# A hybrid attention and DeltaNet layer: weights kept until used, diagonal blocks copied whole, scan products by column halves

## The chip, the cores and the metric

The kernel runs on one core of one Trainium2 chip, as one program. A core has five engines with an instruction stream each: TensorE (PE) for matrix products, with a separate stream of weight loads (PEld); VectorE (DVE); ScalarE (ACT); GpSimd (POOL); SyncE (SP). Each of them takes its instructions in the order in which they stand. SP, ACT and POOL also issue DMA transfers, and a transfer that waits for its data holds up what stands behind it in that queue. The metric is the device time of one execution in microseconds (us); lower is better.

## The reference

One layer of an encoder for 1024 tokens of width 1024. After a conditioned RMSNorm, one projection gives the inputs of two mixers: attention over 8 heads, and a gated DeltaNet with 8 heads that is scanned forwards and backwards in 16 chunks of 64 tokens. A mixture of 16 experts follows. What the change touches is the chunked DeltaNet:

```python
L = where(strict, (kb @ k.T) * decay, 0)          # 64x64, one per chunk, head and direction
T = triangular_solve(eye + L, eye)                # its inverse
u = T @ vb;  w = T @ (kb * exp(gc))
a_intra = where(incl, (q @ k.T) * decay, 0)
...
def step(state, inp):                             # scan over the 16 chunks
    v_new = u_n - w_n @ state
    o_n = qg_n @ state + a_n @ v_new
    state = state * gl_n + kd_n.T @ v_new
```

Both directions run, their outputs are summed, and the sum goes through a gated RMSNorm per head.

## The kernel before

All projections are three products of split weights and activations: `wh`, the rounded weights, with `hTh` and with `hTl`, and `wl`, what the rounding lost, with `hTh`. `proj_load` (L271) asks for a block of 128 columns (`wraw`, a DMA on POOL's queue), rounds it on ACT (`wh`, L278) and subtracts on DVE (`wl`, L279). `wraw`, `wh` and `wl` have two buffers each. A block costs PE 48 products of 128x512 (L285; L1152 in the late filler), and its result leaves through ACT.

The mixer goes through these stages:

1. The DeltaNet's projections, with convolution and normalisation (`dn_group`).
2. `dn_tile` for eight tiles of two chunks: products of keys with keys and with queries (L481), decays (rr on DVE, L489 on PE, the exponential on ACT), and per direction the matrix `at` (stored to `a_d`) and the matrix `nn` (stored to `n_d`, L503). `dn_blocks` then fetches the two 32x32 diagonal blocks of every 64x64 matrix of `n_d` into `nb`, by four DMAs on ACT's queue for each half of the tiles (L511), a row of 32 numbers at a time. Between the tiles stand three projection blocks of queries and keys (`qkv_group`).
3. `dn_invert`: the inverses of all diagonal blocks at once on DVE, 31 steps of two products (L536) and two subtractions (L540), whose size is `q(32-q)` for step `q` in each of two blocks. PE meanwhile has eight projection blocks, `qkv_group` 3 to 5 and `gate_group` 0 to 4 (called gate 0 to gate 4 below). A loop asks for the next block's weights before each:

```python
for n, (f, c, g) in enumerate(fills):
    if n + 1 < len(fills):
        with self.tc.high_priority(offset=0):
            self.proj_ahead(fills[n + 1][1] + fills[n + 1][2] * 128)
    f(g)
```

   `proj_ahead` (L288) keeps a single pair in `self.ahead`. The call for block n+1 comes ahead of block n's use, so it overwrites the pair that was kept for n, and `proj` loads, rounds and subtracts that block a second time. Of the 14 loads of this loop, six are never used.
4. The scan, 16 steps, step t with chunk t forwards and chunk 15-t backwards. `scan_merge` makes the off-diagonal 32x32 blocks of the inverse (L611, L618, 32x32 products, with transposes on DVE, L608). `scan_step` has the products of keys and queries with the state (L633, 128x128, four for each direction), two products on DVE (L636) and two subtractions (L640), the product with the inverse (L645), the state's update (L660, L663, copies on ACT, L666) and the outputs (L670, then sums on DVE, L676 to L679). Between these PE works through the late filler (L1152, 15 blocks), the rotary preparation (`attn_prep`) and the conditioning vector (`mods`).
5. Attention, the merge, the router and the experts.

The order within each engine is set at build time by a list scheduler, from priorities and its own cost estimates; only `dn_invert`'s steps are held in their written order.

## Time and profile before

| | us |
|---|---|
| median of 3 runs | 1736.34 (1730.99 to 1738.34) |
| the profiled execution | 1736.07, its span 1733.9 |
| tile stage | 214 to 291 |
| inversion on DVE | 305.75 to 375.1 |
| last projection block ahead of the late filler ends | 386.2 |
| scan | 408 to 710, late filler until 729 |
| attention, merge, router, experts | to the end |

Over the span PE is busy for 93%, DVE for 84%, ACT for 53%, POOL for 12%; the mean granted TensorE clock is 0.971. These shares are means over very different stages, so a stage has to be read by itself: which engine works without a gap in it, and what the other engines wait for. A busy share of PE includes the time in which a product only drains; how fast PE goes is better read from the distance between the starts of neighbouring rows.

### The profile page before, as it was taken

The numbers are of one execution on the slowest core, as the hardware profiler recorded it, in microseconds if no ns is written. First come the engines' busy times: TensorE is split into PE (matmuls) and PEld (weight loads), VectorE is DVE, ScalarE is ACT, GpSimd is POOL, SyncE is SP. The second block draws the span as 40 slices with busy tenths as digits, with TensorE's granted clock in tenths as the row PEclk, the third lists the DMA queues.
The fourth block names the chain that finished last, engine by engine and source line by source line (L and its number), as shares of the span: only waits on it lengthen the run. The fifth ranks groups of instructions, "written<-read, shape, count | busy, mean of one in ns | idle before, by whom it ended". The sixth has DMA issues, their size and how long they took to land. (4 is left out here: it accounts for less than half of the span.)

```text
span 1733.9 us, 28593 instructions
## 1 busy us (share of the span) xinstructions
PE 1615.1 (93%) x10363; PEld 1287.0 (74%) x10363; DVE 1454.2 (84%) x2523; ACT 924.5 (53%) x1382; POOL 211.9 (12%) x191
## 2 busy tenths in 40 slices
PE   5999998398999999999999999859999999999997
PEld 4777877277777777778887788647777777777776
DVE  6899896966887778889986477979999999999997
ACT  6654522123333323488881223337777777777775
POOL 0011001011111100021113222210010100110000
PEclk9999999699999899999999999969999999999999
DMA  9466479256877876521126463769999999999981
GB/s 279 127 178 187 110 205 221 68 174 174 213 211 189 253 192 159 167 71 37 36 74 202 141 230 128 272 213 345 386 383 371 383 386 383 382 373 382 386 324 25
DMA packets 283052, 390.81 MB, mean 225 GB/s; under 512 B 78299, under 2 KB 151695, under 8 KB 282655
## 3 DMA queue, kind: packets, MB, share of 16 engines
q1 hardware_dynamic: 247103, 328.15, 57.3%
q0 software_dynamic: 12960, 47.19, 9.9%
q10 hardware_dynamic: 22848, 13.63, 2.9%
q8 instruction: 82, 1.34, 0.3%
q14 instruction: 59, 0.48, 0.1%
HBM read 330.14 MB, written 58.77 MB: 224 GB/s over the span
## 5 line engine op out<-in xcount | busy, mean ns | idle before, releaser
L1519 DVE TENSOR_TENSOR ew<-er,ew 128x1024 fp32r<-128x1024 f32 x384 | 452.2, 1220 | 29.8 <-ACT ew L1518 29.8
L1518 ACT CAST ew<-er 128x1024 fp32r<-128x1024 f32 x384 | 391.0, 1048 | 137.9 <-PE pj L1572 108.1
L1572 PE MATMUL pj<-ew,xT 128*128 128x512 f32 x1536 | 367.6, 396 | 4.6 <-DVE ew L1519 4.6
L1572 PEld LDWEIGHTS pj<-ew,xT 128*128 128x128 f32 x1536 | 283.2, 188 | 76.1 <-DVE ew L1519 19.4
L1589 PE MATMUL tr<-ew,aT 128*128 128x512 f32 x768 | 191.4, 398 | 0.0
L1589 PEld LDWEIGHTS tr<-ew,aT 128*128 128x128 f32 x768 | 139.7, 188 | 30.5 <-DVE ew L1519 3.5
L285 PE MATMUL pj<-hTh,wl 128*128 128x512 f32 (+1 forms) x368 | 117.7, 398 | 26.1 <-DVE wl L279 26.1
L285 PE MATMUL pj<-hTh,wh 128*128 128x512 f32 (+1 forms) x368 | 117.2, 398 | 3.6 <-ACT hTh L258 1.8
L285 PE MATMUL pj<-hTl,wh 128*128 128x512 f32 (+1 forms) x368 | 118.6, 399 | 1.4 <-DVE hTl L261 1.4
L278 ACT CAST wh<-wraw 128x1024 fp32r<-128x1024 f32 (+1 forms) x45 | 46.7, 1038 | 126.9 <-PE pj L285 61.1
L285 PEld LDWEIGHTS pj<-hTh,wl 128*128 128x128 f32 (+1 forms) x368 | 69.1, 188 | 43.0 <-DVE wl L279 26.6
L275 POOL DMA_DIRECT2D wraw<-in_w_in_dram x42 | 37.6, 896 | 417.3 <-DVE wl L279 282.3
L1595 POOL DMA_INDIRECT out_dram<-xe,idxT x16 | 37.1, 2316 | 408.5 <-DVE tok L1493 354.0
L841 DVE TENSOR_REDUCE am<-pj 128x1 f32<-128x1024 f32 x64 | 77.8, 1218 | 10.6 <-PE pj L836 10.0
L1198 PE MATMUL pj<-hTh,uw 128*128 128x512 f32 x256 | 83.5, 404 | 1.0 <-DVE uth L1204 0.5
L1152 PE MATMUL pj<-hTh,wh 128*128 128x512 f32 x240 | 82.9, 416 | 0.6 <-ACT y L1157 0.4
L285 PEld LDWEIGHTS pj<-hTh,wh 128*128 128x128 f32 (+1 forms) x368 | 67.9, 187 | 19.6 <-ACT hTh L258 1.9
L1152 PE MATMUL pj<-hTl,wh 128*128 128x512 f32 x240 | 82.1, 411 | 0.0
L1152 PE MATMUL pj<-hTh,wl 128*128 128x512 f32 x240 | 82.1, 410 | 0.0
L285 PEld LDWEIGHTS pj<-hTl,wh 128*128 128x128 f32 (+1 forms) x368 | 68.4, 188 | 17.5 <-DVE hTl L261 2.0
L836 PE MATMUL pj<-kT,qT 128*128 128x512 f32 x256 | 74.9, 403 | 2.3 <-ACT ap L843 1.2
L843 ACT ACTIVATE ap<-pj,am 128x1024 f32<-128x1024 f32 x64 | 72.0, 1125 | 6.7 <-DVE am L841 5.7
(378 smaller groups left out, 3010.1 us busy)
## 6 DMA issues: line engine op xcount, KB each, us to landing
er<-in_w_gate_dram SPq DMA_DIRECT2D x128, 512.0 KB, 7.0
er<-in_w_up_dram SPq DMA_DIRECT2D x128, 512.0 KB
er<-in_w_down_dram SPq DMA_DIRECT2D x128, 512.0 KB, 9.9
wraw<-in_w_in_dram POOLq DMA_DIRECT2D x42, 512.0 KB, 5.9
mw<-in_w_ada_dram SPq DMA_DIRECT2D x64, 256.0 KB, 5.2
wt<-in_w_ada_dram SPq DMA_DIRECT2D x16, 512.0 KB, 8.0
gate_d<-y ACTq DMA_DIRECT2D x32, 256.0 KB, 2.8
kqs<-kq_d SPq DMA_DIRECT2D x32, 256.0 KB, 5.7
```

What stands on the lines that cost most here:

```text
L275: (queue or nc.gpsimd).dma_start(raw[:, :, :n], self.i["w_in"][0, :, col:col + n].rearrange("(k p) c -> p k c", p=128))
L278: nc.scalar.copy(wh[:, :, :n], raw[:, :, :n])
L285: self.nc.tensor.matmul(ps[q][:n], w[:, k, :n], x[k][:, q * 512:(q + 1) * 512], start=(k == 0 and w is wh and x is self.hTh), stop=(k == 7 ...
L836: nc.tensor.matmul(ps[:, kh], qT[:, i * 128:(i + 1) * 128], self.kT[a][:, s, kh * 512:(kh + 1) * 512], start=(s == 0), stop=(s == 1), skip ...
L841: nc.vector.reduce_max(m, ps, axis=AX.X, negate=True)
L843: nc.scalar.activation(p, ps, AF.Exp, bias=m, scale=1.0, accum_out=self.rv[:, h, half * 4 + i:half * 4 + i + 1])
L1152: nc.tensor.matmul(ps[q], a[:, k], x[k][:, q * 512:(q + 1) * 512], start=(k == 0 and a is wh and x is self.hTh), stop=(k == 7 and a is wl))
L1198: nc.tensor.matmul(ps, w[:, k], v[k][:, qs], start=(k == 0 and p == 0), stop=(k == 3 and p == 2))
L1518: nc.scalar.copy(hi, raw)
L1519: nc.vector.tensor_sub(lo, raw, hi.bitcast(F))
L1572: nc.tensor.matmul(pg[m], x[:, 2 * kp + k], wi[:, k], start=(kp == 0 and k == 0 and n == 0), stop=(kp == 3 and k == 1 and n == 2))
L1589: nc.tensor.matmul(py[q], x[:, k], wi[:, q], start=(k == 0 and n == 0), stop=(k == 7 and n == 2))
```

## The change

`self.ahead` becomes a table by column, so a block that was asked for ahead is held until it is used; the eight blocks of stage 3 are loaded once each, the first of them already during the tile stage. Each tile's `nn` goes to DRAM in pieces: the diagonal blocks to `nb_d` (SP, four DMAs for each tile and direction), the one off-diagonal block that is needed to `n_d` (POOL, two). `dn_blocks` fetches whole 8 KB rows of `nb_d` on POOL's queue, after every second tile, in place of ACT's queue. The memset of the inverses moves from POOL to DVE. The transposed diagonal blocks are made once on ACT and stored to `wt_d`, and the scan loads them in place of transposing on DVE. In the scan, the products with the state are split by column halves so that both directions share a PSUM tile: 16 products of 64 columns in place of 8 of 128. Multiplication, subtraction and the sum of outputs are then one instruction for both directions. Outputs are kept by pairs of chunks (t, 15-t), and one output pair is finished in each of the steps 8 to 15.

```diff
     def proj_ahead(self, col):
-        self.ahead = col, self.proj_load(col)
+        self.ahead[col] = self.proj_load(col)
...
-        if self.ahead and self.ahead[0] == col:
-            wh, wl = self.ahead[1]
-            self.ahead = None
-        else:
-            wh, wl = self.proj_load(col, n)
+        wh, wl = self.ahead.pop(col, None) or self.proj_load(col, n)
...
             for x in range(2):
-                nc.sync.dma_start(self.n_d[d, 2 * j + x].rearrange("h s c -> s h c"),
-                                  nn[64 * x:64 * x + 64].rearrange("p (h c) -> p h c", c=64))
+                n = 2 * j + x
+                rows = lambda b, e: nn[64 * x + 32 * b:64 * x + 32 * b + 32].rearrange(
+                    "p (h c) -> p h c", c=64)[:, :, 32 * e:32 * e + 32]
+                for b in range(2):
+                    nc.sync.dma_start(self.nb_d[d, 8 * n:8 * n + 8, b].rearrange("h s c -> s h c"), rows(b, b))
+                nc.gpsimd.dma_start(self.n_d[d, n].rearrange("h s c -> s h c"), rows(d, 1 - d))
...
-            src = self.n_d[d, 2 * j0:2 * j1].rearrange("n h (b s) c -> (n h) b s c", b=2)
-            for b in range(2):
-                self.nc.scalar.dma_start(self.nb[d][16 * j0:16 * j1, b], src[:, b, :, b * 32:b * 32 + 32])
+            self.nc.gpsimd.dma_start(self.nb[d][16 * j0:16 * j1].rearrange("p b s c -> p (b s c)"),
+                                     self.nb_d[d, 16 * j0:16 * j1].rearrange("n b s c -> n (b s c)"))
...
-            nc.gpsimd.memset(w, 0.0)
+            nc.vector.memset(w, 0.0)
...
             nc.sync.dma_start(self.w_d[d], ws[d].rearrange("p b s c -> p (b s c)"))
+            nc.scalar.copy(tmps[d][:, 0], ws[d][:, d].rearrange("p s c -> p c s"))
+            nc.scalar.dma_start(self.wt_d[d], tmps[d][:, 0].rearrange("p c s -> p (c s)"))
...
-        for f, o, cf, co in quads:
-            nc.vector.transpose(wt[f], w[f, :, cf])
...
-        for d, n in enumerate(ns):
-            pk = self.pa.tile([128, 8, 64], F, name="dn", bufs=2)
+        tq = self.tq
+        pk = [self.pa.tile([128, 8, 64], F, name="dn", bufs=2) for _ in range(2)]
+        for y, rows in zip(pk, (rs, os)):
             for p in range(4):
-                nc.tensor.matmul(pk[:, 2 * p:2 * p + 2, :].rearrange("p h c -> p (h c)"), kq[d][:, p],
-                                 self.St[:, d, p, :], start=True, stop=True, skip_group_check=True)
...
+                for d, r in enumerate(rows):
+                    nc.tensor.matmul(y[r, 2 * p:2 * p + 2, :].rearrange("p h c -> p (h c)"), kq[d][:, p, r],
+                                     self.St[:, d, p, :], start=True, stop=True, skip_group_check=True)
+        eg = lambda s: self.egs[:, s, t].unsqueeze(2).to_broadcast([128, 8, 64])
+        nc.vector.tensor_mul(x, pk[0], eg(0))
+        nc.vector.tensor_sub(x, kv[:, 1].rearrange("p (h c) -> p h c", c=64), x)
+        nc.vector.tensor_mul(tq, pk[1], eg(1))
...
-            begin(self.in_turn(self.scan_post(j) for j in range(NT) if max(2 * j + 1, 15 - 2 * j) == t))
+            if t > 7:
+                begin(self.scan_post(15 - t))
...
                     self.dn_tile(j)
-                    if j == 5:
-                        self.dn_blocks(0, 4)
-                self.dn_blocks(4, NT)
+                    if j == QKV[-1]:
+                        self.proj_ahead(C_Q + len(QKV) * 128)
+                    if j in (2, 4, 6):
+                        self.dn_blocks(j - 2, j)
+                self.dn_blocks(6, NT)
```

DVE, between the last tile and the first steps of the inversion: before, with the products on `nb` at L536.

```order
L501 TENSOR_TENSOR nn<-dn,e 128x4x64 x2
L279 TENSOR_TENSOR wl<-wraw,wh 128x1024 x2
L523 MEMSET wb_2752 128x32 x2
L523 MEMSET wb_2757 128x32 x2
L536 TENSOR_TENSOR wtmp_2756<-nb_707,wb_2752 128x2x31
L912 TENSOR_SCALAR macc<-mw_711,cs 128x512
L279 TENSOR_TENSOR wl<-wraw,wh 128x1024
L536 TENSOR_TENSOR wtmp_2761<-nb_708,wb_2757 128x2x31
```

The same place of the changed kernel (its lines 506, 528, 531, 544 are 501, 520, 523, 536 of before; 908 is 902):

```order
L506 TENSOR_TENSOR nn<-dn,e 128x4x64 x2
L279 TENSOR_TENSOR wl<-wraw,wh 128x1024
L528 MEMSET wb_2829 128x2048
L528 MEMSET wb_2834 128x2048
L531 MEMSET wb_2829 128x32 x2
L531 MEMSET wb_2834 128x32 x2
L544 TENSOR_TENSOR wtmp_2833<-nb_709,wb_2829 128x2x31
L908 TENSOR_TENSOR y<-y,tr 1x512
L544 TENSOR_TENSOR wtmp_2838<-nb_710,wb_2834 128x2x31
```

Three `wl` (gate 0's and two that are never used) stand ahead of the second direction's first step before, one (gate 0's) now; two large memsets and the addition L908 have come in.

DVE, around gate 1's `wl` within the inversion (the last two numbers of a shape give the step: 16x16 is step 16), before:

```order
L540 TENSOR_TENSOR wb_2752<-wb_2752,wtmp_2756 128x2x16x16
L540 TENSOR_TENSOR wb_2757<-wb_2757,wtmp_2761 128x2x16x16
L279 TENSOR_TENSOR wl<-wraw,wh 128x1024
L536 TENSOR_TENSOR wtmp_2756<-nb_707,wb_2752 128x2x15x17
L536 TENSOR_TENSOR wtmp_2761<-nb_708,wb_2757 128x2x15x17
```

and now:

```order
L548 TENSOR_TENSOR wb_2829<-wb_2829,wtmp_2833 128x2x19x13
L548 TENSOR_TENSOR wb_2834<-wb_2834,wtmp_2838 128x2x19x13
L279 TENSOR_TENSOR wl<-wraw,wh 128x1024
L544 TENSOR_TENSOR wtmp_2833<-nb_709,wb_2829 128x2x18x14
L544 TENSOR_TENSOR wtmp_2838<-nb_710,wb_2834 128x2x18x14
```

Gate 1's `wl` has moved from behind step 16 to behind step 13; the next three stand behind steps 16, 19 and 22.

PE, a middle step of the scan, from the merge's L618 to the product with the inverse (L645), before:

```order
L618 MATMUL tr<-W,pt 32x32 x16
L1152 MATMUL pj<-hTh_404,wl 128x512
L149 MATMUL tr<-masks,hl 128x128 x4
L1152 MATMUL pj<-hTh_445,wh 128x512
L633 MATMUL dn<-St,kqs 128x128 x2
L149 MATMUL tr<-masks,kk 128x128 x4
L633 MATMUL dn<-St,kqs 128x128 x2
L149 MATMUL tr<-masks,qraw 128x128 x4
L645 MATMUL dn<-st,W 64x64
```

and the same step now (628, 1163, 644 and 657 are 618, 1152, 633 and 645 of before):

```order
L628 MATMUL tr<-W,pt 32x32 x16
L1163 MATMUL pj<-hTh_611,wl 128x512
L149 MATMUL tr<-masks,hl 128x128 x4
L1163 MATMUL pj<-hTh_652,wh 128x512
L644 MATMUL dn<-St,kqs 64x128 x3
L149 MATMUL tr<-masks,kk 128x128 x4
L644 MATMUL dn<-St,kqs 64x128 x11
L149 MATMUL tr<-masks,qraw 128x128 x4
```

The products with the state, full size before, are now two runs of half size between full-size work, and all of a step's stand ahead of the next L645.

## Rows read from the trace of the kernel before

**Rows 1.** Busy time by stage: us (instructions) per engine, granted clock, DMA share.

```profile
core 0: us, PE busy (x) PEld busy (x) DVE busy (x) ACT busy (x) POOL busy (x), PEclk, DMA share, GB/s
214.00:291.00 77.00, 71.50 (x753) 56.10 (x753) 70.85 (x139) 24.82 (x41) 6.38 (x8) 0.96 0.84 209
312.00:339.00 27.00, 1.09 (x4) 0.57 (x4) 27.00 (x53) 2.14 (x3) 0.00 (x0) 0.60 0.12 42
408.00:729.00 321.00, 309.20 (x3611) 244.95 (x3610) 254.64 (x586) 113.07 (x238) 30.22 (x43) 0.98 0.74 196
```

**Rows 2.** Waits, 285 to 400 us: who waited for whom, total, times, longest.

```profile
PE pj L285 <- DVE wl L279: 26.1, 1, 26.1
...
ACT y L896 <- DMA nb<-n_d: 13.2, 1, 13.2
```

**Rows 3.** Timeline of DVE: start, us, instructions, idle before and its releaser.

```profile
280.50 1.23 DVE L279 TENSOR_TENSOR wl<-wraw,wh 128x1024 fp32r<-128x1024 f32 x1 [2.88 <-ACT wh L278]
...
288.62 0.76 DVE L501 TENSOR_TENSOR nn<-dn,e 128x256 f32<-128x256 f32 x2
...
305.75 0.28 DVE L536 TENSOR_TENSOR wtmp<-nb,wb 128x62 f32<-128x62 f32 x1 [7.60 <-DMA nb<-n_d]
...
309.11 0.27 DVE L536 TENSOR_TENSOR wtmp<-nb,wb 128x62 f32<-128x62 f32 x1 [0.33 <-DVE wl L279]
...
330.79 1.26 DVE L536 TENSOR_TENSOR wtmp<-nb,wb 128x504 f32<-128x504 f32 x2
...
337.97 1.21 DVE L279 TENSOR_TENSOR wl<-wraw,wh 128x1024 fp32r<-128x1024 f32 x1
...
374.87 0.34 DVE L540 TENSOR_TENSOR wb<-wb,wtmp 128x62 f32<-128x62 f32 x2
...
392.44 0.91 DVE L570 MEMSET St<- 128x1024 f32 x1 [0.16 <-issue]
```

**Rows 4.** Timeline of PE around gate 1 and where the late filler begins.

```profile
312.47 0.62 PE L285 MATMUL pj<-hTl,wh 128*128 128x512 f32 x2
339.23 1.22 PE L285 MATMUL pj<-hTh,wl 128*128 128x512 f32 x2 [26.14 <-DVE wl L279]
...
386.17 0.61 PE L1152 MATMUL pj<-hTh,wh 128*128 128x512 f32 x2
```

**Rows 5.** Timelines of SP's and ACT's queues: the last stores of `nn`, the second fetch.

```profile
289.40 1.29 SPq L503 DMA_DIRECT2D n_d<-nn  x2
...
291.00 14.05 ACTq L511 DMA_DIRECT2D nb<-n_d  x4
```

**Rows 6.** DMA issues, 230 to 420 us: count, KB each, median us to landing.

```profile
wraw<-in_w_in_dram POOLq DMA_DIRECT2D x17, 512.0 KB, 5.2
...
n_d<-nn SPq DMA_DIRECT2D x28, 128.0 KB, 4.0
```

**Rows 7.** Timeline of PE in the scan; single-precision products (L633, L660) leave two records each.

```profile
468.61 0.62 PE L1152 MATMUL pj<-hTh,wh 128*128 128x512 f32 x2
469.06 0.62 PE L1152 MATMUL pj<-hTl,wh 128*128 128x512 f32 x2
...
470.05 0.68 PE L660 MATMUL tr<-st,kv 64*64 64x64 f32 x16
470.66 0.51 PE L1152 MATMUL pj<-hTh,wl 128*128 128x512 f32 x1
471.09 0.69 PE L618 MATMUL tr<-W,pt 32*32 32x32 f32 x32
...
472.73 0.61 PE L633 MATMUL dn<-St,kqs 128*128 128x128 f32 x4
473.17 0.60 PE L149 MATMUL tr<-masks,kk 128*128 128x128 f32 x4
```

**Rows 8.** Longest waits of PE, 408 to 729 us.

```profile
PE dn L645 <- DVE st L640: 3.1, 1, 3.1
PE tr L149 <- DVE Sc L663: 3.1, 1, 3.1
```

More of the change, by code (lines that the diff above doesn't have):

```diff
@@ L406, in dn_gates @@
         nc.scalar.copy(flat[:, 1], e)
-        eg = self.ab.tile([128, NT, 2, 16], F, name="eg")
+        eg = sp.tile([128, NT, 2, 16], F, name="eg", tag="sq", bufs=1)
         gl = a.rearrange("p j (x e) -> p j x e", x=2)
@@ L435, in dn_gates @@
             nc.scalar.copy(gls[:, :, d * 4:d * 4 + 4], turn(gl[:, :, d * 4:d * 4 + 4]))
-        self.eg, self.gls, self.dk = eg, gls, dk
+        egs = self.ab.tile([128, 2, 16, 8], F, name="egs")
+        ev = eg.rearrange("p j x e -> p (j x) e")
+        for x in range(2):
+            for s in range(2):
+                lo, hi = (slice(64 * y, 64 * y + 64) for y in ((x + s) % 2, (1 - x + s) % 2))
+                nc.scalar.copy(egs[lo, s, x::2, :], ev[lo, x::2, 0:8])
+                nc.scalar.copy(egs[hi, s, x::2, :], rev1(ev[hi, 1 - x::2, 8:16]))
+        self.egs, self.gls, self.dk = egs, gls, dk
     def dn_scalars(self):
         nc, sp = self.nc, self.ap
-        nc.scalar.copy(self.ssqs[0:64], self.ssq[64:128])
-        nc.scalar.copy(self.ssqs[64:128], self.ssq[0:64])
+        for x in range(2):
+            here, there = slice(64 * x, 64 * x + 64), slice(64 - 64 * x, 128 - 64 * x)
+            nc.scalar.copy(self.ssqs[there, x::2], self.ssq[here, 0:4])
+            nc.scalar.copy(self.ssqs[there, 1 - x::2], rev1(self.ssq[here, 4:8]))
         rk2 = sp.tile([128, NT, 8], F, name="rk2", bufs=1)
@@ L586, in scan_load @@
             src = self.w_d[d].rearrange("(n h) (b s c) -> n b s h c", h=8, b=2, s=32)
-            nsrc = self.n_d[d, n].rearrange("h (b s) (e c) -> b s h e c", b=2, e=2)[d, :, :, 1 - d, :]
+            nsrc = self.n_d[d, n].rearrange("h s c -> s h c")
             for b in range(2):
@@ L969, in scan @@
             fill(FILL[3])
[L970 removed]
+            if t > 7:
+                begin(self.scan_post(15 - t))
             some(2)
@@ L1003, in mixer @@
             self.a_d = dnp.tile([2, NT, 128, 512], F, name="a_d")
-            self.n_d = dnp.tile([2, 16, 8, 64, 64], F, name="n_d")
+            self.n_d = dnp.tile([2, 16, 8, 32, 32], F, name="n_d")
+            self.nb_d = dnp.tile([2, 128, 2, 32, 32], F, name="nb_d")
             self.w_d = dnp.tile([2, 128, 2048], F, name="w_d")
+            self.wt_d = dnp.tile([2, 128, 1024], F, name="wt_d")
             self.qkv_d = dnp.tile([6, 128, S], F, name="qkv_d")
@@ L1016, in mixer @@
             self.pa = self.pool(self.root, "pa", space=PSUM)
-            self.ahead = None
+            self.ahead = {}
             self.lo = nc.vector
@@ L1078, in mixer @@
             t = self.unit("g17", (128, 2, 512), name="mw")
-            self.mod_tiles([t[:, n] for n in range(2)], self.unit("g18", (128, 2, 512), name="macc"))
+            self.mod_tiles([t[:, 0], t[:, 1], self.mw2], self.unit("g18", (128, 2, 512), name="macc"))
             self.more = self.mods(MODG, 8)
```

48 lines of the change are left out of this document (19 added, 29 removed).

## The prediction, made before the result was known

> **What bounds the kernel now.** I read the busy times by stage first, then the waits, then the timelines of the engines that wait for each other, and last the queues that carry the diagonal blocks. In the tile stage DVE is busy for 70.85 of 77 us and PE for 71.50, so neither can give much alone [rows 1]. In the next stage the reader is to see an exchange: from 312 to 339 DVE works without a gap and PE for 1.09 us, at a granted clock of 0.60. The one wait behind it is the longest of the stretch: PE has the rest of its projections to do and stands 26.1 us for gate 1's `wl` [rows 2]. The timeline gives its ends, 313.1 and 339.23; after it PE works through four blocks until 386.17, 11.7 us each, and then the late filler [rows 4]. In the scan and the filler PE is busy for 309.20 of 321 us, DVE for 254.64 [rows 1]. So PE is the bound from 339 to 729 and a `wl` that comes sooner moves all of that forward, up to the 26 us of the wait.
>
> Why does that `wl` come at 337.97? DVE takes its instructions in order, and it stands behind step 16 of the inversion. The inversion in turn began late: the first L536 at 305.75 had waited 7.60 us for `nb`, and the second direction's first step, from which the steps run without waits, began at 309.11 [rows 3]. The fetch of `nb` for the second half of the tiles occupied ACT's queue for 14.05 us from 291.00, directly behind the last stores of `nn` (289.40 to 290.69) [rows 5]. ACT's next instruction stood 13.2 us behind it [rows 2].
>
> **The change, part by part.** The sum is made against the profiled execution, 1736.07 us (span 1733.9, so 2.2 outside it); the median of the runs is 1736.34, so the two are interchangeable here.
>
> *Tile stage.* The scheduler has 14 loads in this loop before, eight now. Of those ahead of the last tile's `nn`, three `wl` of 1.23 us leave DVE, 3.7 us, and with them the 2.88 us for which DVE waited for a `wh` [rows 3]. That would be 6.6 us, but PE has only 77 - 71.5 = 5.5 us of slack there. Between 3.7 and 5.5 I take 4.5: the last `nn`, which ends at 288.62 + 0.76 = 289.4 [rows 3], then ends at 284.9. The lower bound is no gain, if PE's 5.5 us are waits in other places. The moves of small copies to ACT I cost at nothing: ACT is busy for 24.82 of 77 us [rows 1]. SP gets more to issue: two stores took 1.29 us [rows 5], so 0.65 each; four for each tile and direction are 2.6, with the store of `at` some 3 us in a period of 77 / 16 = 4.8. It still keeps up; three more stores and it would not, and then `nn`, which has two buffers, would hold DVE.
>
> *Start of the inversion.* Two paths have to be ready. On DVE: from 284.9 gate 0's `wl` (1.2) and the two memsets that come from POOL. A memset of 1024 columns took 0.91 us [rows 3], so one of 2048 takes 1.8 and both 3.6: ready at 289.7. By DMA: the last four stores are issued by 284.9 + 2.6 = 287.5, land 4.0 later [rows 6], 291.5; then the fetch on POOL's queue. Its duration isn't in the trace. It is one transfer with 8 KB in a row, so its nearest row is `wraw`, 5.2 us from issue to landing for 512 KB [rows 6]; the far bound is the 14.05 us of the old fetch. I take 5.2, as the reason for the 14 us, rows of 32 numbers, is gone. With 0.9 for the second direction's issue, its first step starts at 291.5 + 5.2 + 0.9 = 297.6 in place of 309.11: 11.5 us sooner. The memsets are hidden behind this DMA path; without it they would cost 3.6. With 14.05 in place of 5.2 it is 306.3, 2.8 sooner. With no DMA time at all, DVE's path gives 290, 19 sooner.
>
> *Gate 1's `wl`.* It now stands behind step 13. Step 14 began at 330.79 and the `wl` behind step 16 at 337.97 [rows 3], so it moves forward by a further 7.2 us. The addition that stood between the first steps has gone ahead of them, some 0.6. Sum: 11.5 + 7.2 + 0.6 = **19.3 us sooner**, 339.2 becomes 319.9. PE's earlier work would end some 4.5 sooner, 308.6, so it still waits 11 us. What is late next? The blocks after it take 11.7 each, so gate 2's `wl` is wanted at 331.6; it stands three steps on, at most 7.2 + 1.2 later on DVE, 328.3, and the next ones likewise gain on PE, as the steps shrink. The late filler starts at 366.9 in place of 386.17, and DVE's inversion, 375.2 before [rows 3], ends at 375.2 - 11.5 - 0.6 - 1.2 = 361.9 (five `wl` stand within it before, four now); the first late block's `wl` stands right behind its end, so it comes some 3 us ahead of need. Bounds of this term: 2.8 + 7.2 + 0.6 = 10.6, if the fetch is no quicker; 19 + 7.2 + 0.6 = 27, if only DVE counts, where PE's wait is all but gone.
>
> *Products with the state.* Before, 8 products a step, two records each, in 16 steps: 256 records. Four took 473.17 - 472.73 = 0.44 us, 0.11 each [rows 7], together 28.2 us. Now there are 512 of half the columns of weights and no row shows one. Its nearest row is L660: 64x64, neighbouring products on the same 64 rows and in alternating column halves, 16 records in 0.61 us, 0.038 each [rows 7]. By that 512 take 19.5. The runs are cut more often by full-size work; the order has 54 more changes between full-size and split products. A full-size L1152 ahead of one of these took 471.09 - 470.66 = 0.43 where one among its like takes 0.225 [rows 7], 0.2 for a change, 54 x 0.2 = **5.4**, not taken for nothing since no wait hides it. Together 24.9 for 28.2: **-3.3**. Bounds: halves wholly side by side 14.1 + 5.4 = 19.5, -8.7; one after the other at the old 0.11 a record 56.3 + 5.4 = 61.7, **+33**. I take 0.038, since it is the one row with alternating column halves on shared rows.
>
> The Trainium skill, page "TensorE: Matmul & The Clock Gate", Part 3, under "What overlaps and what doesn't", says that a weight load overlaps with products in flight only where its group of rows differs. Both halves use all 128 rows, so by that rule the change would pay for its loads, towards the +33. The rows of L660, which share their rows and take 0.038 a record, speak against it; this decides a rival below.
>
> *The rest of the scan.* DVE loses transposes, a subtraction and sums, and it isn't the bound (254.64 of 321). The longest waits of PE there are 3.1 us, for the subtraction L640 and for the state [rows 8]. Both directions now share one subtraction, so the first direction waits for the second's products; on the other side fewer instructions stand ahead. I take nothing, between -6.2 (both waits gone) and +1 a step, 16 us, where a step has no filler between the products with the state and L645. The transposed blocks on ACT and their store stand beside PE's filler, as do the wasted loads that go (ACT 113.07 of 321 busy, DMA share 0.74): nothing.
>
> Sum: 1736.1 - 19.3 - 3.3 = **1713.5**.
>
> **Rivals.** (a) *The blocks come no sooner.* POOL's fetch stands behind the stores of the off-diagonal blocks on the same queue and may wait for them; or writing 32 numbers in a row costs at the store what it cost at the fetch. For it: the 14.05 us of four DMAs with such rows. Against it: the `n_d` stores of 64 in a row land in 4.0. 1736.1 - 10.6 - 3.3 = 1722.
>
> (b) *The scan gives it back.* Products of both directions ahead of one subtraction leave PE with nothing for about a microsecond a step: 1713.5 + 16 = 1729.5. For it: the split products of a step stand right ahead of L645 in the order. Against it: DVE's shorter work in each step.
>
> (c) *Slower: the column halves run one after the other.* -19.3 + 33 gives 1750. The kernel is slower from the record r at which 512 x r + 5.4 - 28.2 exceeds 19.3: r = 0.082 us. L660 says 0.038, but on half of the rows.
>
> (d) *All of it.* The fetch is hidden, the gate opens when DVE can (-27), the halves run side by side (-8.7), and the two waits of 3.1 vanish: 1694.
>
> That the change doesn't do what it says is excluded by the order: the `wl` of gate 1 stands three steps earlier.
>
> **How the numbers follow.** Forecast 0.55, (a) 0.15, (b) 0.11, (c) 0.08, (d) 0.11. The predicted time is the forecast's, 1713. For 8 in 10, (c) and the far part of (d) are left out: 1697 to 1730. A measurement can tell some 0.5%, 8.7 us, from no change. Forecast, (a) and (d) are faster by more, 0.81; (b) lies within, 0.11; (c) is slower, 0.08.
>
> **What would show it.** After: PE's wait for gate 1's `wl` of 9 to 13 us, with its end near 320; the first L536 of the second direction (now L544) near 297; the late filler from 367. A wait of more than 18 says rival (a), and the fetch's landing time says why. In the scan, a run of split products (now L644) with starts 0.04 us a record apart, and the distance from one run's start to the full-size work behind it, show the product term; 0.1 a record would be (c). The scan's length beside its filler, 408 to 729 before, should be 3 us shorter at the same work; longer waits of PE at the subtraction would be (b). I am wrong if PE's wait has only moved to a later `wl`, or if the tile stage doesn't end sooner.

## The result: slower by 1.4%

The changed kernel takes 1760.05 us (median of 4 runs, 1754.59 to 1762.93) against 1736.76 of the kernel before: a ratio of 1.014, with a 95% interval of 1.0117 to 1.0163. The forecast was 1713, its range ended at 1730, and slower had a chance of 0.08. The profiled execution took 1754.59 us, its span is 1752.8.

The first half of the reasoning holds in the trace. The waits of the changed kernel, 285 to 400 us (engine, line and what it waited for; total, times, longest):

```profile
PE pj L285 <- DVE wl L279: 9.7, 1, 9.7
```

Before it was 26.1 [rows 2]; the forecast left 11. So the wait shrank as forecast, and no later `wl` took its place. The timeline of DVE (start, us, instructions, idle before and its releaser):

```profile
289.00 0.76 DVE L506 TENSOR_TENSOR nn<-dn,e 128x256 f32<-128x256 f32 x2 [2.74 <-DMA nb_d<-nn]
...
291.26 1.76 DVE L528 MEMSET wb<- 128x2048 f32 x1 [0.38 <-issue]
...
298.24 0.27 DVE L544 TENSOR_TENSOR wtmp<-nb,wb 128x62 f32<-128x62 f32 x1 [2.82 <-issue]
...
299.35 0.28 DVE L544 TENSOR_TENSOR wtmp<-nb,wb 128x62 f32<-128x62 f32 x1 [0.26 <-DMA nb<-nb_d]
...
320.43 1.22 DVE L279 TENSOR_TENSOR wl<-wraw,wh 128x1024 fp32r<-128x1024 f32 x1
```

Gate 1's `wl` starts at 320.43 in place of 337.97 [rows 3]. The second direction's first step starts at 299.35, 9.8 sooner. PE:

```profile
321.71 1.22 PE L285 MATMUL pj<-hTh,wl 128*128 128x512 f32 x2 [9.67 <-DVE wl L279]
...
371.36 0.62 PE L1163 MATMUL pj<-hTh,wh 128*128 128x512 f32 x2
```

The late filler begins at 371.4, 14.8 us ahead of before [rows 4]. Its last products, now and then before:

```profile
745.71 0.72 PE L1163 MATMUL pj<-hTh,wl 128*128 128x512 f32 x2
```

```profile
728.60 0.64 PE L1152 MATMUL pj<-hTh,wl 128*128 128x512 f32 x2
```

They end at 746.4, before at 729.2. So the stretch of scan and filler grew from 343 to 375 us, and here lies the loss: -14.8 + 32.0, and 1.7 behind it, make the 18.9 between the two spans.

What PE does in it is best seen at the first of three pockets. The timeline of PE (L1163 is the filler, L644 the products with the state, L621 and L628 the merge, L657 the product with the inverse):

```profile
521.61 0.62 PE L1163 MATMUL pj<-hTh,wl 128*128 128x512 f32 x2
522.16 0.68 PE L672 MATMUL dn<-st,kv 64*64 64x64 f32 x16
523.24 1.15 PE L682 MATMUL dn<-st,sa 64*64 64x64 f32 x32 [0.40 <-PE dn L672]
527.32 0.76 PE L621 MATMUL tr<-Sc 32*32 32x32 f32 x32 [2.93 <-DVE xnq L758]
528.01 0.44 PE L644 MATMUL dn<-St,kqs 128*64 128x128 f32 x4
532.05 1.09 PE L149 MATMUL tr<-masks,hl 128*128 128x128 f32 x4 [3.60 <-DVE hl L771]
533.06 1.12 PE L672 MATMUL tr<-st,kv 64*64 64x64 f32 x16
534.12 1.06 PE L628 MATMUL tr<-W,pt 32*32 32x32 f32 x32
...
541.26 1.11 PE L657 MATMUL dn<-st,W 64*64 64x64 f32 x30 [0.94 <-DVE st L648]
...
544.85 0.73 PE L1163 MATMUL pj<-hTh,wh 128*128 128x512 f32 x2 [1.26 <-ACT y L1168]
```

For 23 us there is no filler. What is left is the chain of a step, PE to DVE to PE; and behind the first gaps L672, L628 and L149 take over one and a half times as long (L672 1.12 us for 16 records at 533.06, 0.68 at 522.16). The busy times of the eight us behind these gaps and of the three pockets (us and instructions for each engine, then granted clock, DMA share and GB/s):

```profile
core 0: us, PE busy (x) PEld busy (x) DVE busy (x) ACT busy (x) POOL busy (x), PEclk, DMA share, GB/s
532.00:540.00 8.00, 7.95 (x88) 6.18 (x90) 1.42 (x3) 3.31 (x7) 1.61 (x4) 0.58 0.59 152
522.00:545.00 23.00, 13.87 (x215) 10.66 (x214) 13.86 (x36) 8.66 (x18) 2.51 (x5) 0.78 0.72 186
623.00:640.00 17.00, 11.56 (x171) 8.38 (x170) 8.81 (x14) 4.53 (x9) 0.88 (x1) 0.80 0.77 187
700.00:723.00 23.00, 15.23 (x269) 12.00 (x270) 14.98 (x37) 8.41 (x18) 0.00 (x0) 0.85 0.65 150
```

Over each pocket neither PE nor DVE is busy for more than 70%, and the mean granted clock is 0.78 to 0.85: part of the time at 1.2 GHz. From 532 to 540 it is 0.58, with PE busy throughout.

The table is worked out from the PE rows of each kernel: the stretch from the start of the first to the end of the last product of the late filler; PE's idle time in it (gaps over 0.1 us); what two kinds of products take from start to next start, without such gaps; and how many of the filler's 720 products stand ahead of step 5's first product with the state. The names below the first two are those of the experiments. The ratio is of all runs, the rest of the one execution that was profiled; for the changed kernel, e_wt_pool and e_extra_loads this one was the fastest, some 5 us below the median, and for e_blocks, which has no row here, the slowest.

| kernel | ratio (95%) | filler from, to | stretch | idle | with the state | L645, L657 | filler ahead of step 5 |
|---|---|---|---|---|---|---|---|
| before | | 386.2, 729.2 | 343.1 | 16.5 | 31.1 | 22.2 | 267 |
| changed | 1.0140 (1.0117 to 1.0163) | 371.4, 746.4 | 375.1 | 33.3 | 39.3 | 18.4 | 312 |
| e_first_half | 0.9954 (0.9931 to 0.9977) | 372.1, 721.9 | 349.8 | 21.0 | 31.1 | 22.5 | 285 |
| e_scan_half | 1.0209 (1.0158 to 1.0261) | 386.8, 763.6 | 376.8 | 32.9 | 39.3 | 18.5 | 303 |
| e_whole | 1.0096 (1.0068 to 1.0124) | 372.8, 750.3 | 377.5 | 38.0 | 33.9 | 20.1 | 306 |
| e_direct | 1.0099 (1.0069 to 1.0129) | 373.8, 746.1 | 372.4 | 31.2 | 37.7 | 18.6 | 312 |
| e_old_step | 1.0139 (1.0102 to 1.0176) | 375.3, 756.0 | 380.7 | 33.3 | 38.8 | 22.6 | 307 |
| e_own_transpose | 0.9946 (0.9923 to 0.9969) | 373.6, 719.7 | 346.1 | 16.4 | 36.4 | 17.8 | 282 |
| e_wt_pool | 1.0040 (1.0015 to 1.0065) | 371.5, 726.4 | 354.9 | 18.2 | 37.7 | 18.2 | 279 |
| e_wt_double | 1.0143 (1.0098 to 1.0187) | 374.2, 749.9 | 375.6 | 31.5 | 39.6 | 18.5 | 312 |
| e_extra_loads | 1.0101 (1.0062 to 1.0139) | 369.7, 738.5 | 368.8 | 30.6 | 38.3 | 18.8 | 311 |
| e_old_step_transpose | 1.0001 (0.9980 to 1.0023) | 374.4, 725.4 | 351.0 | 20.5 | 31.6 | 22.5 | 285 |
| e_fewer_issues | 0.9980 (0.9960 to 1.0001) | 375.0, 725.4 | 350.4 | 16.0 | 38.6 | 17.6 | 247 |

### The profile page after: what moved, and what is told of

It reads as the page before. It is cut to its first block, busy times and chain, and to the rows that moved or that the text cites. A ratio compares the mean times of both kernels' runs of the same rounds, so it can differ in the third digit from the quotient of the medians.

```text
span 1752.8 us, 29190 instructions
## 1 busy us (share of the span) xinstructions
PE 1633.1 (93%) x10619; PEld 1290.4 (74%) x10619; DVE 1409.3 (80%) x2439; ACT 927.2 (53%) x1388; POOL 224.3 (13%) x223
## 5 line engine op out<-in xcount | busy, mean ns | idle before, releaser
L278 ACT CAST wh<-wraw 128x1024 fp32r<-128x1024 f32 (+1 forms) x39 | 40.4, 1037 | 135.1 <-PE pj L285 98.4
L1163 PE MATMUL pj<-hTh,wh 128*128 128x512 f32 x240 | 82.3, 412 | 5.2 <-ACT y L1168 2.3
L1163 PE MATMUL pj<-hTl,wh 128*128 128x512 f32 x240 | 82.5, 413 | 0.0
L1163 PE MATMUL pj<-hTh,wl 128*128 128x512 f32 x240 | 82.2, 413 | 0.0
L285 PEld LDWEIGHTS pj<-hTl,wh 128*128 128x128 f32 (+1 forms) x368 | 68.8, 188 | 17.8 <-DVE hTl L261 2.0
L275 POOL DMA_DIRECT2D wraw<-in_w_in_dram x36 | 32.6, 905 | 366.4 <-DVE wl L279 215.2
```

The costliest lines, as they stand in the source:

```text
L278: nc.scalar.copy(wh[:, :, :n], raw[:, :, :n])
L285: self.nc.tensor.matmul(ps[q][:n], w[:, k, :n], x[k][:, q * 512:(q + 1) * 512], start=(k == 0 and w is wh and x is self.hTh), stop=(k == 7 ...
L1163: nc.tensor.matmul(ps[q], a[:, k], x[k][:, q * 512:(q + 1) * 512], start=(k == 0 and a is wh and x is self.hTh), stop=(k == 7 and a is wl))
```

## The experiments

### Which half of the change

The first half is the table of weights asked for ahead and the way of the diagonal blocks, on the old scan; the second half is the new scan alone.

> The kernel before with the first half of the change alone: the table of weights asked for ahead, the diagonal blocks in whole pieces, the memsets on DVE. The scan is the old one. Theory A (the loss of 32 us between the start of the late filler and its end belongs to the new scan): the late filler starts near 371 as in the changed kernel, the scan and the filler take 343 us as before, so 1736 - 15 = 1721 us. Theory B (the scan cannot use an earlier start, because its pace from about 495 us on is set by something that the first half doesn't touch, and idle time takes the gain back): 1733 to 1738 us, with 12 to 17 us more idle time of PE between 371 and 730 than before.

Measured: 1730.1 us, ratio 0.9954, some 8 us faster. The filler starts where it does in the changed kernel, and ends 7.3 sooner than before. Half of the 14 us is lost in the scan, between the two theories; of the 6.7 us by which its stretch is longer, 4.5 are idle time of PE.

> The kernel before with the second half of the change alone: the new scan (products by column halves, joint instructions, outputs by pairs, transposed blocks made on ACT), with the old weights ahead and the old fetch of the blocks. Theory A: it loses all of the 32 us, 1736 + 30 = 1766 us (1760 to 1772). Theory B: the scan loses only what its products cost, 8 us, so 1744 us.

Measured: 1772.9 us, ratio 1.0209. The new scan alone loses it all, and a little more than theory A said; its stretch is 376.8 us, with the same 33 us of idle time.

The parts of the first half one by one: `self.ahead` as a table with the first block asked for during the tile stage; and the stores, the fetch and the memsets.

> The kernel before with the table of weights asked for ahead alone; the blocks go the old way, over ACT's queue. By the terms of the prediction, gate 1's wl comes sooner by its place three steps earlier (7.2 us) and little for the loads that go, 330 in place of 339; in the first half of the change together it came at 321, 17.5 us sooner, and 8 of these were left at the end. So 1731 to 1735 us. Rival (each part alone does nothing, because the other wait then holds): 1736 to 1739 us, the wl at 337 or later.

> The kernel before with the diagonal blocks in whole pieces on POOL's queue and the memsets on DVE alone; the weights asked for ahead are overwritten as before. By the terms of the prediction the inversion starts some 10 us sooner and gate 1's wl stays behind step 16, near 329; 1731 to 1735 us. Rival (the unused loads on DVE take up the time between the tiles and the first step, and the wl hardly moves): 1736 to 1739 us.

Measured: 1730.8 us (0.9966, 0.9953 to 0.9980) and 1731.9 us (0.9977, 0.9960 to 0.9994). PE's wait for gate 1's `wl`, in the timeline of PE with the table alone:

```profile
330.06 1.22 PE L285 MATMUL pj<-hTh,wl 128*128 128x512 f32 x2 [18.68 <-DVE wl L279]
```

and with the blocks alone:

```profile
351.87 1.22 PE L285 MATMUL pj<-hTh,wl 128*128 128x512 f32 x2 [23.16 <-DVE wl L279]
```

The table moves gate 1's first product by 9.2 us, as the terms said. In the traced execution of the blocks alone it doesn't come sooner: the unused loads stay on DVE, the last `nn` begins at 299.44 in place of 288.62, and the first step of the second direction at 314.08. But this execution took 1740.2 us, the slowest of ten, and the other nine 1729.2 to 1735.8. So its trace shows only that this one began the filler late, at 392.0; where the median's 4 us come from, and whether the `wl` came sooner in the nine, isn't shown. The expectation met the number, and its mechanism is open.

### The products and the step of the scan

What the split products cost was read from runs of each form by itself:

```diff
+        forms = [[(128, c, 128) for _ in range(8) for c in (None, None)],
+                 [(128, c, 128) for _ in range(16) for c in H],
...
+            for n, (k, c, m) in enumerate(f):
...
+                nc.tensor.matmul(y[:, n % 4 * 128:n % 4 * 128 + m], self.St[0:k, 0, n % 4, c], self.St[0:k, 1, n % 4, 0:m],
```

> The kernel before with 176 single-precision products added ahead of the scan whose results are used for nothing: runs of 16 or 32 of one form, in the order (rows of weights x columns of weights, columns moved): 128x128, 128; 128x64 in alternating column halves, 128; the same, 64 moved; 64x64 in alternating halves, 128 moved; the same, 64 moved; 128x64 in one half only, 128 moved; 128x128, 64 moved. To be read: the distance of the starts, two records each product. Theory A (halves run in pairs, and a pair takes as long as its moved columns ask, whatever the rows): a pair of records 0.11 us at 128 moved and 0.058 us at 64, with 128 rows or 64. Rival (a pair's time goes with the rows of weights to load): 0.11 with 128 rows and 0.06 with 64, whatever is moved. One half only: 0.11 a record by theory A, that is twice the time per product.

Each product leaves two records, 384 in all. Distances of the starts of neighbouring records, us; the last column is the time from a run's first start to the start of what follows it, for each of its products:

| rows x columns of weights, columns moved | distances | per product |
|---|---|---|
| 128x128, 128 | 0.112, 0.111 | 0.229 |
| 128x64, halves in turn, 128 | 0.006, 0.103 | 0.111 |
| 128x64, halves in turn, 64 | 0.007, 0.052 | 0.061 |
| 64x64, halves in turn, 128 | 0.006, 0.102 | 0.111 |
| 64x64, halves in turn, 64 | 0.007, 0.052 | 0.061 |
| 128x64, one half only, 128 | 0.109 | 0.223 |
| 128x128, 64 | 0.112, 0.111 | 0.225 |

Two halves start within 7 ns of each other, whatever their rows. The pair then takes, to the start of the next, what its moved columns ask: 0.109 for 128, 0.058 for 64. So 16 products of half the columns take what 8 whole ones took: theory A, and its rival falls. In the kernel the row is the same (PE, step 0):

```profile
403.07 1.75 PE L644 MATMUL dn<-St,kqs 128*64 128x128 f32 x28 [0.54 <-DMA kqs<-kq_d]
404.75 0.72 PE L1163 MATMUL pj<-hTl,wh 128*128 128x512 f32 x2
```

28 records in 1.68 us are 0.060 each, 14 pairs of 0.109 and the way out. Before, four whole records took 0.44 [rows 7].

Then the products whole again in the changed kernel, first with the joint subtraction, then with the whole old step:

```diff
+        for d, y in enumerate(pk):
             for p in range(4):
-                for d, r in enumerate(rows):
-                    nc.tensor.matmul(y[r, ...], kq[d][:, p, r], ...
+                nc.tensor.matmul(y[:, ...], kq[d][:, p], ...
```

> The changed kernel with the products of keys and queries with the state whole again: 8 of 128 columns in place of 16 of 64, and the multiplications with the decays on half the partitions, four in place of two; all else as changed. Theory A (two halves side by side take 0.109 us, as long as one whole record, 0.110, because either moves 128 columns of state; and the cuts between halves and full-size work cost 0.1 us each way): PE gets back the 8.2 us by which these products grew, the idle pockets of the scan stay, 1760 - 8 = 1752 us. Rival A2 (the idle time of the scan comes from the joint subtraction that waits for the products of both directions): unchanged by this, 1757 to 1762 us, or more for two more instructions on DVE.

> The changed kernel with the step of the scan as it was: 8 whole products, and for each direction its own multiplication, subtraction and sums. What stays of the new scan: the outputs by pairs of chunks, and the transposed blocks that come by DMA. Theory C (the step itself costs: products by halves 8 us net, and all of them in one run of both directions between the state and the joint subtraction, so that the chain of a step is longer where the filler is used up): 1760 - 22 to 30, 1730 to 1738 us, and under 24 us of idle time from the filler's start to its end. Theory D (outputs by pairs and the loads of transposed blocks leave PE idle): 1750 us or more, 30 us of idle time stay.

```diff
-        nc.vector.tensor_sub(x, kv[:, 1]..., x)
+        for d, n in enumerate(ns):
...
+            nc.vector.tensor_mul(tp, pk, self.eg[:, n // 2, n % 2, d * 8:d * 8 + 8]...)
+            nc.vector.tensor_sub(x[r], kv[r, 1]..., tp[r])
```

Measured: 1756.1 us (1.0096) and 1762.7 us (1.0139). The first lies between its two theories: PE gets 5.4 us back, but idles for 38.0 in place of 33.3. In the second theory C falls: with the old step nothing comes back. So neither the split products nor the joint instructions are needed for the pockets.

### The pockets and the y buffers

At each pocket the filler had to stop, as its results leave through two `y` buffers, in which the conditioning vector has its turn at steps 6, 10 and 14.

```diff
-            for s, t in enumerate((hi, lo)):
-                nc.tensor.matmul(ps[0:1], self.one, t, start=(s == 0), stop=(s == 1))
+            nc.tensor.matmul(ps[0:1], self.ones[:, 0:1], acc, start=True, stop=True)
```

> The changed kernel with one thing else: in the scan the conditioning vector's sum over partitions is one single-precision product straight from its accumulator, in place of two products of a rounded half and its rest, so that these two halves no longer occupy both of the y buffers through which the late filler's results leave. Theory A3 (the pockets of idle time at 522 to 545, 620 to 640 and 700 to 725 stand at the ends of the stretches in which both y buffers are held, 500.2 to 538.4, 592.4 to 632 and 677.7 to 709.6, because the filler can't go on there): most of the 17 us of idle time and of the 6 us at half clock go, 1738 to 1745 us. Rival A2 (joint subtraction, chain of the scan's own steps): the pockets stay, 1756 to 1761 us.

Measured: 1756.0 us (1.0099). The pockets stay where they are. The bias row still used a `y` buffer, so the wall stood; the next run took that away too (`mb = self.mw2[0:1]`).

> The changed kernel with the conditioning vector taken out of the y buffers altogether in the scan: its sum is one single-precision product straight from the accumulator, and its bias row lies in the third buffer of the conditioning weights, of which two are left. In the run before this one the bias row still took its turn among the y buffers, and the filler's results still waited for it at the same three places (blocks 8, 12 and 15 of the filler began at 546, 640 and 723, as in the changed kernel). Theory A3 (the filler has a wall at three steps of the scan, where the conditioning vector has its turn in the y buffers; it reaches the wall 15 us sooner than before, and PE then has only the scan's chain to work on): without the wall the filler goes on, no pocket of more than 3 us is left in 520 to 725, and the time is 1738 to 1746 us. Rival A2 (the scan's own chain, with joint instructions that wait for both directions, is what leaves PE idle, wall or no wall): 30 us of idle time stay and 1753 to 1760 us.

Measured: 1745.6 us, ratio 1.0057 (1.0039 to 1.0074). The filler has no pocket, and PE idles for 10.2 us until its end. But this end comes at 690, and steps 13 to 15 then have 8, 0 and 0 filler products and take 19, 18 and 12 us; before, with 26, 24 and 20, they took 15, 14 and 15. So without the wall 14 of the 23 us go, though as many filler products stand ahead of step 5 as in the changed kernel, 312. The wall puts a date on the loss and makes part of it; what is left fits filler that is used up too early.

> The first half of the change with the old scan, and the conditioning vector out of the y buffers in the scan (one single-precision product, bias row in a buffer of the scan's outputs). The first half alone started the filler 14 us sooner and ended 8 us sooner. Theory A3: the wall took the rest; without it 1720 to 1725 us. Rival A2 (the old scan's chain has its own limit): 1728 to 1732 us.

> The kernel before with the same thing done to the conditioning vector in the scan. Theory A3 (the wall costs when the filler comes to it early, and here it comes when the wall opens): no change within 4 us, 1734 to 1741 us. Rival A4 (the wall costs the kernel before as well, some 9 us of its 16.5 us of idle time): 1727 to 1731 us.

Measured: 1733.5 us (0.9985, 0.9965 to 1.0004) and 1734.9 us (0.9992, 0.9974 to 1.0010). The second is as A3 said. The first isn't: without the wall the first half alone is no better, if not worse. Its bias row lies in a buffer of the scan's outputs, which may cost something of its own. What takes half of the gain is not shown to be the wall, and it stays open.

### The transposed blocks

The one edit left is that the scan loads the transposed diagonal blocks. Undone:

```diff
-            nc.sync.dma_start(self.wt[f], self.wt_d[d].rearrange("(n h) (c s) -> n c h s", h=8, s=32)[n])
...
+        for f, o, cf, co in quads:
+            nc.vector.transpose(wt[f], w[f, :, cf])
```

> The changed kernel with the diagonal blocks transposed on DVE in the scan, as before, in place of the copies on ACT, their store and the loads. All else of the new scan stays. Theory C: the loads cost the 4.1 us that PE waits for them and DVE has room for the transposes, 1754 to 1760 us. Theory D: 1745 us or less.

Measured: 1726.9 us, ratio 0.9946: theory D. This one edit costs 33 us, and without it the changed kernel is faster than before. Busy times of the scan in this kernel:

```profile
408.00:720.00 312.00, 300.89 (x3739) 227.57 (x3738) 222.94 (x534) 111.17 (x231) 27.00 (x43) 1.00 0.74 196
```

and of the changed kernel to its filler's end:

```profile
408.00:747.00 339.00, 312.97 (x3741) 238.04 (x3742) 212.80 (x506) 113.47 (x236) 25.73 (x43) 0.95 0.73 185
```

Almost the same number of PE instructions, 27 us apart, at a granted clock of 1.00 and 0.95. The DVE work that the loads take away is 10 us. The loads, the copies on ACT and their store came and went together; no run has the copies alone.

How do two loads of 32 KB a step cost 33 us? PE's waits for them in the changed kernel, 408 to 747:

```profile
PE tr L621 <- DMA Sc<-wt_d: 3.0, 3, 1.5
```

That is no 33. Four runs were made on it. The loads issued by POOL; two buffers for them; the loads given back to the good kernel, into a buffer that nothing reads; and the loads of the off-diagonal blocks moved from SP to POOL in the good kernel.

```diff
-            nc.sync.dma_start(self.wt[f], self.wt_d[d]...)
+            nc.gpsimd.dma_start(self.wt[f], self.wt_d[d]...)
```

> The changed kernel with the loads of the transposed blocks issued by POOL in place of SP; the same loads, the same single buffer, nothing else. The order that the scheduler makes of it has 279 products of the late filler ahead of step 5's first product with the state, against 312 in the changed kernel, 282 with the transposes on DVE and 267 before. Theory O (the two issues more for each step on SP's queue, which by the scheduler's estimates make the loads of a step late, let it pull more filler ahead of each step; the filler is used up before the scan ends, and the chain of a step then stands alone on PE): the loss goes with the order, 1725 to 1735 us. Rival L (the transposed blocks come late by the chip's clock, or their loads disturb others, and PE waits): 1750 us or more.

Measured: 1740.6 us, ratio 1.0040, between the two theories. The stretch falls from 375 to 355 us and the idle time from 33.3 to 18.2; two pockets of some 12 us are left in place of three of 16 to 24. Of the 33 us 19 go with the order, though the loads are the same. The other 14 stay, though the order has as few products ahead of step 5 (279) as e_own_transpose (282): theory O doesn't explain them. The copies, the store, the loads themselves and the issue on POOL are left as causes, untested one by one.

```diff
-            nc.sync.dma_start(self.wt[f], self.wt_d[d]...)
+            nc.sync.dma_start(self.wts[t % 2][f], self.wt_d[d]...)
```

> The changed kernel with two buffers for the transposed blocks, so that their load need not wait for the merge of the step before; the second buffer takes the place of the third buffer of the conditioning weights. The order of PE's instructions is that of the changed kernel, product by product of the filler. Theory O: the order stays and so does the loss, 1754 to 1761 us. Rival L: the 4.1 us of waits for the blocks and what follows from them go, 1740 us or less.

Measured: 1760.3 us, ratio 1.0143: the same order, the same loss. It tells less than was meant: PE's waits for the blocks stayed too (3.9 us), since the loads stand on SP's queue behind stores (`qT_d` and `kT_d`) and not behind the merge.

```diff
-            nc.sync.dma_start(self.wt[f], self.wt_d[d]...)
+            nc.sync.dma_start(self.mw2[f, 0:256]..., self.wt_d[d]...)
+        for f, o, cf, co in quads:
+            nc.vector.transpose(wt[f], w[f, :, cf])
```

> The kernel with the transposes back on DVE (1727 us), to which the two loads for each step on SP's queue are given back, into a buffer that nothing reads. Nothing on PE depends on them. The order has 311 products of the filler ahead of step 5. Theory O: the order alone brings the loss back, 1748 to 1762 us. Rival L (the merge's dependence on the loaded blocks is what costs): 1727 to 1733 us.

Measured: 1750.7 us, ratio 1.0101. Loads that nothing waits for, with their copies and store, bring back 24 of the 33 us. The buffer that they fill was the third one of the conditioning weights, which are left two; e_old_step_transpose below has two as well and 285 products ahead of step 5, so this alone doesn't move the filler. PE's longest waits there, 408 to 739 us:

```profile
PE tr L623 <- DVE Sc L620: 5.8, 3, 3.0
PE tr L623 <- DVE xnq L760: 4.7, 2, 3.5
PE tr L149 <- DVE hl L773: 3.7, 1, 3.7
```

Its busy times in the same stretch:

```profile
408.00:739.00 331.00, 307.00 (x3716) 235.19 (x3714) 221.06 (x529) 111.66 (x231) 25.92 (x43) 0.95 0.73 187
```

The loads aren't among the causes of these waits. The clock is at 0.95 again, the idle time at 30.6, and the filler stands as in the changed kernel: 311 products ahead of step 5, with pockets at 520 to 543, 619 to 634 and 692 to 716. This is what theory O says: what costs is the place of the filler in the order that the scheduler made. Order and loads came back together here, so the share of each has to be taken from both runs: with the loads and without the order 19 of the 33 us go, with both and without a wait for the loads 24 come back. Somewhat over half of the loss goes with the order; the rest isn't settled. That the two issues enter its estimates as a late end of SP's queue is inferred from the orders; the estimates themselves were not read.

```diff
-            nc.sync.dma_start(nf[f], nsrc)
+            nc.gpsimd.dma_start(nf[f], nsrc)
```

> The kernel with the transposes back on DVE (1727 us), with the two loads of the off-diagonal blocks for each step issued by POOL in place of SP. Nothing else. The order goes the other way than in the changed kernel: 247 products of the filler ahead of step 5 (282 with the loads on SP, 312 changed), 434 ahead of step 10 (508), and 96 behind the last step (38). Theory O (the issues on SP's queue set by the scheduler's estimates how much filler goes early, and early filler is what the scan lacks later): the idle time of 16 us falls to some 10 and the time to 1717 to 1723 us. Rival (the loss had to do with the transposed blocks alone): 1725 to 1730 us, or more by the slower issue of POOL.

> The same with the conditioning vector out of the y buffers in the scan as well (one single-precision product, its bias row in the third buffer of the conditioning weights). 247 products of the filler ahead of step 5, 444 ahead of step 10, 96 behind the last step, and no step has fewer than 30. Theory A3 with theory O: no wall and filler in every step, 1713 to 1720 us. Rival (the wall costs only where the filler comes to it early, which it no longer does): as the run beside it, within 3 us.

Measured: 1733.3 us (0.9980) and 1729.9 us (0.9965, 0.9941 to 0.9989). Theory O falls in this direction. The filler is spread as it said, but the idle time stays (16.0), and the filler's own products take 193.1 us in place of 188.4; they are cut by other products more often (125 runs in place of 115). So 312 ahead of step 5 goes with a loss while the wall stands, 247 is no better than 282, and the count alone doesn't give the time.

Last, the step of the scan in the good order:

> The kernel with the transposes back on DVE (1727 us) and the step of the scan as it was: whole products, and for each direction its own multiplication, subtraction and sums. Of the new scan only the outputs by pairs of chunks stay. The order has 285 products of the filler ahead of step 5, against 282. By the theory on the products (halves side by side save nothing, 0.109 us a pair against 0.111 a whole record, and the cuts cost): PE gets back some 5 us, 1719 to 1724 us. Rival (joint instructions on DVE and the shorter chain are worth that): 1727 to 1732 us.

Measured: 1734.9 us, ratio 1.0001: the rival. The halves do cost PE 36.4 against 31.6 us. But with the joint subtraction a step's records of the product with the inverse stand in one run (17 runs in 16 steps, against 31), and take 17.8 us against 22.5; and the old step waits more:

```profile
PE dn L649 <- DVE st L644: 6.1, 2, 4.8
```

So the new step, split products and all, is worth 8 us.

This kernel is e_first_half with the outputs by pairs, and little else. That had 0.9954 (0.9931 to 0.9977), this has 1.0001: the outputs by pairs, beside the old step, cost 5 to 8 us. No run says why, and the prediction had no term for them.

## Why the prediction was wrong, step by step

Of the 47 us between the forecast and the result, 33 belong to the transposed blocks, their copies, store and loads: without them the changed kernel takes 1726.9 us, inside the range of 1697 to 1730. That this lies inside is partly luck. The first half gives 8 us in place of 19.3; the new step gives 8, though its products cost time; and the outputs by pairs cost 5 to 8, with no term in the sum.

**Gate 1's `wl`**: right in sum (19.3 forecast, 17.5 measured), with two errors that nearly cancel. The tile stage was to end 4.5 us sooner and ended at 289.8, 0.4 later: where three unused `wl` left DVE, it waited 2.74 us for the stores of `nn` instead. The prediction named this wait and put it three stores away; the row shows it there. And the DMA path was quicker than 4.0 + 5.2: from the last `nn` to the second direction's first step 9.6 us, against 12.7.

**What is late next**: missed in part. The late filler started 14.8 sooner, not 19.3, since PE then waited for the conditioning vector (2.9 us until 353.80) and worked at 1.2 GHz behind that wait too (granted clock 0.62 from 354.0 to 358.5). Worse, "all of that moves forward" failed: in e_first_half, 14 us at the start of the filler are 8 at the end. The prediction took PE busy for 309 of 321 us as proof that PE's work is the whole length. The pockets of the changed kernel show that it is not: there the scan is a chain that looks hidden only while filler is left to lie beside it. Which steps take the 6 us in e_first_half is open.

**Products with the state**: the term of -3.3 was mis-sized; it measured +8.2 in the changed kernel (31.1 to 39.3 us) and +4.8 in the good order (31.6 to 36.4). The row L660 moves 64 columns, and L633 moves 128; the prediction took its 0.038 us a record for its "alternating column halves on shared rows" and left the moved columns out. At 128 a pair costs 0.109 (e_forms): no gain. Rival (c), one after the other at 0.11 a record, falls as well. The 5.4 for the changes is a slip, as 54 x 0.2 is 10.8; with it the term would have been +2.1 and the sum 1718.9. That 5.4 is nearer to what is left over is luck: a change costs about half of 0.2. In e_own_transpose a filler product ahead of a run of halves takes 0.32 to the next start, among its like 0.23:

```profile
522.47 0.39 PE L1162 MATMUL pj<-hTl,wh 128*128 128x512 f32 x1
522.79 0.44 PE L643 MATMUL dn<-St,kqs 128*64 128x128 f32 x4
```

The Trainium skill, page "TensorE: Matmul & The Clock Gate", Part 3, under "What overlaps and what doesn't", says that a weight load overlaps with products in flight only where its group of rows differs. Here halves on the same 128 rows start 6 ns apart and a pair takes 0.109 or 0.058 as its moved columns go, so its loads add nothing; one half alone takes 0.109 a record. The measurement decides: column halves overlap.

**The transposed blocks**: this is the step that decided. The sentence was that the blocks on ACT and their store "stand beside PE's filler": nothing. It weighed the copies and the store and forgot the two loads a step that the scan got in return, on SP's queue. The price is 33 us by e_own_transpose; PE's waits for the loads in the changed kernel are 3.0. Somewhat over half of it goes with the order, which has 312 filler products ahead of step 5, without the loads 282 and before 267; the rest stays open. The change of the order could have been seen without a time: the order of PE of the changed kernel has 76, 41, 47, 51, 45 and 52 filler products ahead of steps 0 to 5, before 60, 33, 37, 44, 47 and 46; and then 24 and 6 in steps 5 and 14, where before had 40 and 24.

**The rest of the scan**: "longer waits of PE at the subtraction" (b) did not come; L657 waits 2.8 us for it. Rival (b) had the right place, a step without filler, and the wrong reason and size.

**Chances**: 0.81 for faster rested on one mechanism and counted the scan as one product term. No rival said that the order itself might change for the worse.

## What to carry to other kernels

Where a scheduler fills a long chain with independent work, the length of that stretch is not the sum of its work: count, from the order, how much filler each step gets, before and after, and look for steps that get little or none. A count ahead of one step is a hint, not a price: 247, 282 and 312 gave 1733, 1727 and, by whether the wall stood, 1760 or 1746 us. An edit that takes work from an engine with room and puts two DMA issues a step on a busy queue can cost far more through the order than through any wait it adds (here 19 of 33 us went with the order, and the waits were 3.0). Price a product by the columns that it moves as well as by the weights that it loads, and take the price from a row that agrees in both.

## What the runs showed of the hardware

Products on the two column halves of the array run in pairs, 6 to 7 ns apart, with the same 128 rows or with 64. From pair to pair it is 0.109 us with 128 columns moved and 0.058 with 64. The two records of a whole 128x128 product are 0.112 and 0.111 us apart with 64 columns moved and with 128: there fewer moved columns save nothing. So splitting by columns halves the time of a product that moves 64 columns, and gives nothing at 128.

A short stop has an echo: after the pocket's gaps of 2.93 and 3.60 us PE's small products took over one and a half times as long (L628 1.06 us for 32 records at 534.12; before, as L618, 0.69 [rows 7]), at a granted clock of 0.58 from 532 to 540. The scan's mean granted clock was 0.95 there, and 1.00 in e_own_transpose.
